# First block's attention: the second score product with 128 rows, the keys' low parts kept in both halves

## The chip, the core and the metric

The kernel runs on one core of a Trainium2 chip. Its engines run in parallel, each through its own instructions in order: TensorE (PE; the loading of its weights is shown as PEld), VectorE (DVE), ScalarE (ACT), GpSimd (POOL) and SyncE (SP, which issues the DMAs). They wait for each other by semaphores. The metric is device microseconds of one execution, the median of several runs. Lower is better.

## What is computed

256 latent tokens `x` and 256 context tokens `ctx`, of width 1024, go through a first block of two layers, then the latents alone through a second block (forgetting attention, an LRU, a mixture of 32 experts). Each layer of the first block has three branches, merged under gates:

```
s = einsum('btgrd,blgd->bgrtl', q, k) * 64 ** -0.5      # 2 key heads g, 4 query heads r for each
p = softmax(s, axis=-1)
y_attn = einsum('bgrtl,blgd->btgrd', p, v) * silu(a_g)
y_gla  = gla_finish(forward scan + backward scan) * silu(g_g)
mixed  = einsum('gts,bnsgc->bntgc', w_s, layer_norm(s_v)) + b_s
y_sgu  = s_u * mixed * silu(s_g)
m   = sigmoid(m_a) * (y_attn @ w_br_attn) + sigmoid(m_g) * (y_gla @ w_br_gla) + sigmoid(m_s) * (y_sgu @ w_br_sgu)
out = m @ w_out
```

Latents attend to the context and themselves (512 keys), context tokens to the context alone (256 keys). The second layer needs only the latents' output. All is fp32.

## The kernel before

Every fp32 operand of a large product is split into a high and a low part, and a product is made as high by high, high by low and low by high; lines 228, 229 and 230 are these three for one tile of a weight (`whi`, `wlo`) and of the transposed activations (`hTh`, `hTl`), with as many columns as there are tokens (512 in layer 0, 256 in layer 1). Lines 97 and 98 split the weights.

A layer runs its branches and then the merge, and a scheduler sets each engine's order: it takes an instruction when its inputs and its buffer are there by its own estimate. Buffers come from rings that are given out in the order of the program's text, a ring's next user waits for the one as many places before it as the ring has buffers. So work of a later function can stand between the steps of an earlier one wherever it has its inputs and buffers. The text's order in a layer ends with the GLA scan (`gops`, its finish with L846 on POOL and the transposes `tro`, L849), `attn_core`, `sgu_core`, and `merge`.

*Attention* (`attn_core`): for each tile of 128 queries (four in layer 0: two of latents, two of context; two in layer 1) four rounds `r` of two heads `g`. A round makes the scores `asc` in two PSUM banks, each by two products: the queries' high and low halves, stacked in `qs` over 128 rows, by the keys' high part `kh`, which is kept in both halves of the rows (L609); and the queries' high half by the keys' low part `kl`, over 64 rows (L611). Then come the maximum (L616, DVE), the exponential (L619, ACT), the division (L620, L621, DVE), four transposes (`trp`, L624, PE), their copy (`pt`, L626, ACT) and the weighting of the values (`aops`, L631, PE). After four rounds the tile is gated as `yt` (L635, DVE), and split into `yat`.

*SGU* (`sgu_core`): four products `mxps` for each tile of 128 tokens (L913), in a bank of the PSUM ring "gm", which has two; DVE takes them out into `mx` (L917, four instructions), POOL multiplies (L920), ACT and DVE split the result into `ysg` (L921, L922).

*Merge* (`merge`): twelve steps, each with gate products `mgps`, which need only the layer's input, and branch products `brps`. Their banks come from the same ring "gm" (in layer 1's attention steps the branch products take another).

In layer 1, POOL also prepares the residual with the layer norm's constants `post`, between the two heads of the last GLA pair (L1132, L1133), when they have been loaded.

Of the kernel before, what the change touches and what calls it, by code (L numbers as in the profile page):

```python
# [10 lines left out]
F32 = mybir.dt.float32  # L11
F32R = mybir.dt.float32r
# [3 lines left out]
OP = mybir.AluOpType  # L16
# [59 lines left out]
class Builder:  # L76
# [409 lines left out]
    def attn_tiles(self):  # L486
        L = self.L
        a1 = self.slot.tile([128, 2, 4, self.nx], F32, tag=self.half, bufs=self.nhalf, name="a1")
        L["a1"] = a1
        L["qT"], L["agT"] = a1[:, 0], a1[:, 1]  # L490

        L["kh"] = self.akv.tile([128, 2, 512], F32R, tag="kh", name="kh")
        L["kl"] = self.akv.tile([128, 512], F32R, tag="kl", name="kl")
        L["v"] = self.akv.tile([128, 4, 128], F32, tag="v", name="v")

    def attn_kv(self, t0, t1):
        nc, a, L = self.nc, self.a, self.L
        kh, kl, v = L["kh"], L["kl"], L["v"]
        tts = range(t0 // 128, t1 // 128)
        g = self.gemm_tok(self.chunk(a["w_in"][self.li], C_AK), tts)  # L500
        for tt in tts:
            kt = self.att.tile([128, 512], F32, tag="att2k", name="ktok")[:, :128]
            nc.scalar.activation(v[:, tt], g[tt][:, 128:256], AF.Copy)
            self.norm_rope(g[tt][:, 0:128], 2, 1, tt, kt.rearrange("p (h e) -> p h e", e=64))
            ps = self.ptr.tile([128, 128], F32, tag="tr", name="trk")
            nc.tensor.transpose(ps, kt, self.ident)
            ts = slice(tt * 128, tt * 128 + 128)
            for h in range(2):
                pr, other = slice(64 * h, 64 * h + 64), slice(64 - 64 * h, 128 - 64 * h)
                nc.scalar.activation(kh[pr, h, ts], ps[pr], AF.Copy)  # L510
                nc.vector.tensor_tensor(kl[pr, ts], ps[pr], kh[pr, h, ts].bitcast(F32), op=OP.subtract)
                nc.gpsimd.tensor_copy(kh[other, h, ts], kh[pr, h, ts])

    def attn_q(self):
        nc, a, L = self.nc, self.a, self.L
        w = a["w_in"][self.li]
        nq = self.nx // 128
        a1, qT = L["a1"], L["qT"]
        qtok = {}
        for c in range(2):  # L520
            g = self.gemm_tok(self.chunk(w, C_AQ + 256 * c), range(nq))
            for tt in range(nq):
                if c == 0:
                    qtok[tt] = a1[:, 1].rearrange("p r t -> p (r t)")[:, 512 * tt:512 * tt + 512].rearrange(
                        "p (r g e) -> p r g e", r=4, g=2)
                self.norm_rope(g[tt], 4, 0, tt, qtok[tt][:, :, c])
        for tt in range(nq):
            ps = self.ptr.tile([128, 4, 128], F32, tag="tr", name="trq")
            for r in range(4):
                nc.tensor.transpose(ps[:, r], qtok[tt][:, r].rearrange("p g e -> p (g e)"), self.ident)  # L530
            nc.scalar.activation(qT[:, :, tt * 128:tt * 128 + 128], ps, AF.Copy)
# [57 lines left out]
    def attn_core(self):  # L589
        nc, L = self.nc, self.L  # L590
        nq = self.nx // 128
        qT, kh, kl, v = L["qT"], L["kh"], L["kl"], L["v"]
        halves = [slice(64 * g, 64 * g + 64) for g in range(2)]
        y = L["y_a"] = self.slot.tile([128, 2, 4, self.nx], F32R, tag="slot", name="yat")
        for tt in range(nq):
            keys = (0, 512) if tt < 2 else (256, 512)
            nk = keys[1] - keys[0]
            nkc = nk // 128
            ops = self.pou.tile([128, 4, 128], F32, tag="ou", name="aops")

            qs = self.att.tile([128, 4, 2, 128], F32R, tag="qs", name="qs")
            for g in range(2):
                src, hi = qT[halves[g], :, tt * 128:tt * 128 + 128], qs[halves[g], :, g]
                nc.scalar.activation(hi, src, AF.Copy)
                nc.vector.tensor_tensor(qs[halves[1 - g], :, g], src, hi.bitcast(F32), op=OP.subtract)
            for r in range(4):
                sc = [self.psc.tile([128, 512], F32, tag="sc", name="asc")[:, :nk] for g in range(2)]
                for g in range(2):
                    nc.tensor.matmul(sc[g], qs[:, r, g], kh[:, g, keys[0]:keys[1]], start=True, stop=False)  # L609
                for g in range(2):  # L610
                    nc.tensor.matmul(sc[g], qs[halves[g], r, g], kl[halves[g], keys[0]:keys[1]], start=False, stop=True)  # L611
                pts = []
                for g in range(2):
                    s = sc[g]
                    st = self.sm.tile([128, 4], F32, tag="ast", name="ast")
                    nc.vector.tensor_reduce(st[:, 0:1], s, axis=AX.X, op=OP.max)  # L616
                    nc.vector.tensor_scalar(st[:, 1:2], st[:, 0:1], -0.125, None, op0=OP.mult)
                    p = self.att.tile([128, 512], F32, tag="att2k", name="p")[:, :nk]
                    nc.scalar.activation(p, s, AF.Exp, scale=0.125, bias=st[:, 1:2], accum_out=st[:, 2:3])  # L619
                    nc.vector.reciprocal(st[:, 3:4], st[:, 2:3])  # L620
                    nc.vector.tensor_scalar(p, p, st[:, 3:4], None, op0=OP.mult)  # L621
                    tp = self.ptr.tile([128, 4, 128], F32, tag="tr", name="trp")
                    for k in range(nkc):
                        nc.tensor.transpose(tp[:, k], p[:, k * 128:k * 128 + 128], self.ident)  # L624
                    pt = self.att.tile([128, 4, 128], F32, tag="pt", bufs=2, name="pt")
                    nc.scalar.activation(pt[:, :nkc], tp[:, :nkc], AF.Copy)  # L626
                    pts.append(pt)

                for k in range(nkc):
                    for g in range(2):  # L630
                        nc.tensor.matmul(ops[halves[g], r], v[:, keys[0] // 128 + k, 64 * g:64 * g + 64], pts[g][:, k],  # L631
                                         start=(k == 0), stop=(k == nkc - 1), skip_group_check=True)
            t = self.tmp.tile([128, 4, 128], F32, tag="tmp", name="yt")
            tc = slice(tt * 128, tt * 128 + 128)
            nc.vector.scalar_tensor_tensor(t, ops, 0.5, L["agT"][:, :, tc], op0=OP.mult, op1=OP.mult)  # L635
            nc.scalar.activation(y[:, 0, :, tc], t, AF.Copy)
            nc.vector.tensor_tensor(y[:, 1, :, tc], t, y[:, 0, :, tc].bitcast(F32), op=OP.subtract)
# [269 lines left out]
    def sgu_core(self):  # L907
        nc, L = self.nc, self.L
        y = L["y_s"]
        for tt in range(self.nx // 128):  # L910
            ps = self.pgm.tile([128, 4, 128], F32, tag="gm", name="mxps")
            for g in range(4):
                nc.tensor.matmul(ps[:, g], L["vn"][:, tt, g * 128:g * 128 + 128], L["wsT"][:, g], start=True, stop=True,  # L913
                                 skip_group_check=True)
            t = self.att.tile([128, 4, 128], F32, tag="mx", bufs=1, name="mx")
            for g in range(4):
                nc.vector.scalar_tensor_tensor(t[:, g], ps[:, g], L["vT"][:, 28 + g:29 + g], L["sgr"][:, g],  # L917
                                               op0=OP.mult, op1=OP.add)
            tc = slice(tt * 128, tt * 128 + 128)
            nc.gpsimd.tensor_tensor(t, t, L["su"][:, :, tc], op=OP.mult)  # L920
            nc.scalar.activation(y[:, 0, :, tc], t, AF.Copy)  # L921
            nc.vector.tensor_tensor(y[:, 1, :, tc], t, y[:, 0, :, tc].bitcast(F32), op=OP.subtract)  # L922
# [1048 lines left out]
```

## Time and profile before

| | before |
|---|---|
| median of 3 runs | 1337.82 us (1337.48 to 1339.54) |
| the profiled execution | 1342.17 us, span 1339.8 us |
| granted TensorE clock, mean | 0.981 |
| busy in the span | PE 1262.4 us (94%), DVE 724.2 (54%), ACT 577.9 (43%), POOL 334.9 (25%) |

The span is from the first to the last instruction of the profiled execution; busy is the time in which an engine had an instruction in work. A matmul's shown duration is longer than the distance to the next one, since they are pipelined; the distance of the starts tells what one costs.

### The profile page before, as it was taken

Reading aid. Unit: us, or ns where it says so; the run is one execution under the profiler, and the core shown is the slowest. Engines: PE = TensorE matmul, PEld = TensorE weight load, DVE = VectorE, ACT = ScalarE, POOL = GpSimd, SP = SyncE. Lnnn points to the kernel's source line nnn. Section 1 sums busy time; section 2 is a strip of 40 time slices with the busy share of each in tenths; the row PEclk is TensorE's granted clock in tenths of the full one; section 3 lists DMA queues with packets and bytes.
Section 4 is the critical chain, followed back from the end, with each engine's and each line's share of the span. In section 5 each row is a group of like instructions: output and inputs, shape, how many; then the busy total and the mean of one; then the engine's idle time right before and its main releaser. Section 6 shows DMA issues by size and latency. Waiting matters only on the chain.

```text
span 1339.8 us, 22959 instructions
## 1 busy us (share of the span) xinstructions
PE 1262.4 (94%) x8819; PEld 977.2 (73%) x8819; DVE 724.2 (54%) x1428; ACT 577.9 (43%) x1115; POOL 334.9 (25%) x373
## 2 busy tenths in 40 slices
PE   6999999999999999999999999999899989999975
PEld 3789888777777766799989988799898675333311
DVE  2565585775443323378768877646878455111112
ACT  2463454455343222346776554545465333222201
POOL 2237645340001101242246545002124020000000
PEclk9999999999999999999999999999899799999998
DMA  9613222211124676545555546246498546999994
GB/s 320 188 53 110 74 58 79 65 48 48 48 75 132 188 252 221 173 149 167 152 149 157 138 116 186 67 126 193 123 327 252 187 174 257 409 408 409 408 409 185
DMA packets 182165, 243.89 MB, mean 182 GB/s; under 512 B 15284, under 2 KB 154780, under 8 KB 182048
## 3 DMA queue, kind: packets, MB, share of 16 engines
q1 hardware_dynamic: 182048, 242.35, 54.9%
q8 instruction: 71, 1.16, 0.4%
q14 instruction: 46, 0.38, 0.1%
HBM read 241.27 MB, written 1.05 MB: 181 GB/s over the span
## 4 chain that ended last, share of the span: by engine, by line
PE 65%; DMA 15%; DVE 8%; ACT 4%; issue 3%; POOL 2%; SPq 1%; ACTq 0%; DVEq 0%; POOLq 0%
DMA gu<-w_up 7%; PE mgps L228 5%; PE mgps L230 5%; PE mgps L229 5%; PE gmt L263 4%; PE gmt L264 4%; PE gmt L265 4%; PE gups L1737 3%; DVE wlo L98 2%; DMA dn<-w_down 2%; DMA raw<-w_in 2%; PE brps L228 2%; PE brps L229 2%; PE brps L230 2%; PE aops L631 2%
## 5 line engine op out<-in xcount | busy, mean ns | idle before, releaser
L98 DVE TENSOR_TENSOR wlo<-raw,whi 128x1024 fp32r<-128x1024 f32 (+1 forms) x202 | 253.5, 1261 | 156.7 <-ACT whi L97 153.8
L97 ACT ACTIVATE whi<-raw 128x1024 fp32r<-128x1024 f32 (+1 forms) x216 | 212.5, 993 | 199.3 <-PE mgps L229 41.8
L264 PE MATMUL gmt<-wlo,hTh 128*128 128x256 f32 x480 | 138.0, 288 | 2.5 <-DVE wlo L98 2.5
L263 PE MATMUL gmt<-whi,hTh 128*128 128x256 f32 x480 | 137.3, 287 | 2.1 <-DVE a L587 0.9
L265 PE MATMUL gmt<-whi,hTl 128*128 128x256 f32 x480 | 137.3, 286 | 0.0
L228 PE MATMUL mgps<-hTh,whi 128*128 128x512 f32 (+1 forms) x384 | 132.0, 345 | 0.0
L229 PE MATMUL mgps<-hTl,whi 128*128 128x512 f32 (+1 forms) x384 | 130.6, 340 | 0.0
L230 PE MATMUL mgps<-hTh,wlo 128*128 128x512 f32 (+1 forms) x384 | 130.4, 342 | 0.0
L957 POOL TENSOR_TENSOR msum<-msum,tanh 128x512 f32<-128x512 f32 (+1 forms) x32 | 36.8, 1154 | 329.7 <-DVE tanh L956 310.2
L1737 PE MATMUL gups<-gu,xw 128*64 128x512 f32 (+1 forms) x512 | 97.5, 603 | 8.4 <-DMA gu<-w_up 8.4
L264 PEld LDWEIGHTS gmt<-wlo,hTh 128*128 128x128 f32 x480 | 92.6, 193 | 5.9 <-DVE wlo L98 2.9
L263 PEld LDWEIGHTS gmt<-whi,hTh 128*128 128x128 f32 x480 | 92.5, 193 | 3.9 <-ACT g L669 1.1
L265 PEld LDWEIGHTS gmt<-whi,hTl 128*128 128x128 f32 x480 | 92.7, 193 | 2.3 <-issue 2.2
L228 PEld LDWEIGHTS mgps<-hTh,whi 128*128 128x128 f32 x384 | 72.6, 189 | 12.9 <-issue 5.0
L230 PEld LDWEIGHTS mgps<-hTh,wlo 128*128 128x128 f32 x384 | 72.5, 189 | 10.2 <-issue 2.5
L229 PEld LDWEIGHTS mgps<-hTl,whi 128*128 128x128 f32 x384 | 72.7, 189 | 9.0 <-issue 2.0
L1737 PEld LDWEIGHTS gups<-gu,xw 128*64 128x64 f32 (+1 forms) x512 | 25.3, 124 | 62.0 <-issue 60.0
L203 POOL TENSOR_TENSOR frs<-rsq,mhalf 128x1 f32<-128x1 f32 x2 | 1.1, 549 | 234.7 <-DVE frs L1911 234.7
L1769 DVE SCALAR_TENSOR_TENSOR eth<-eth,gups 128x256 f32<-128x256 f32 x12 | 5.1, 421 | 99.8 <-ACT eth L1768 99.8
L1792 PE MATMUL dnps<-dn,hm 128*64 128x512 f32 (+1 forms) x256 | 52.2, 599 | 6.2 <-DMA dn<-w_down 6.0
L264 PE MATMUL gmt<-wlo,mm 128*128 128x256 f32 x192 | 54.5, 285 | 0.6 <-DVE wlo L98 0.6
L263 PE MATMUL gmt<-whi,mm 128*128 128x256 f32 x192 | 54.1, 285 | 0.0
(559 smaller groups left out, 3109.2 us busy)
## 6 DMA issues: line engine op xcount, KB each, us to landing
raw<-w_in SPq DMA_DIRECT2D x132, 512.0 KB
gu<-w_gate SPq DMA_DIRECT2D x64, 512.0 KB
gu<-w_up SPq DMA_DIRECT2D x64, 512.0 KB
dn<-w_down SPq DMA_DIRECT2D x28, 1024.0 KB
adar<-w_ada SPq DMA_DIRECT2D x32, 512.0 KB
raw<-w_out SPq DMA_DIRECT2D x32, 512.0 KB
adaw<-w_ada SPq DMA_DIRECT2D x16, 512.0 KB
raw<-w_in SPq DMA_DIRECT2D x32, 256.0 KB
```

Of the source, the lines that this page charges most:

```text
L97: nc.scalar.activation(hi, x, AF.Copy)
L98: return (eng or nc.vector).tensor_tensor(lo, x, hi.bitcast(F32), op=OP.subtract).ins
L228: nc.tensor.matmul(ps, wh, xh, start=(u == 0 and k == 0), stop=False)
L229: nc.tensor.matmul(ps, wh, xl, start=False, stop=False)
L230: nc.tensor.matmul(ps, wl, xh, start=False, stop=(u == len(acts) - 1 and k == 3))
L263: nc.tensor.matmul(out[tt], xh, hi[:, j, :n], start=first, stop=False, skip_group_check=True)
L264: nc.tensor.matmul(out[tt], xh, lo[:, j, :n], start=False, stop=False, skip_group_check=True)
L265: nc.tensor.matmul(out[tt], xl, hi[:, j, :n], start=False, stop=last, skip_group_check=True)
L631: nc.tensor.matmul(ops[halves[g], r], v[:, keys[0] // 128 + k, 64 * g:64 * g + 64], pts[g][:, k], start=(k == 0), stop=(k == nkc - 1), ski ...
L957: nc.gpsimd.tensor_tensor(sums[c, j], sums[c, j], ts[j], op=OP.add)
L1737: mm = nc.tensor.matmul(u["ps"][pr], u["x"][:, k, pr], u["gu"][ei][k // 4][:, :, k % 4], start=(k == 0), stop=(k == 7), skip_group_check=T ...
L1792: mm = nc.tensor.matmul(ps[pr], hm[:, f, pr], dns[ei][:, f, 512 * hf:512 * hf + 512], start=(f == 0), stop=(f == 1), skip_group_check=True ...
```

## The change

The keys' low part `kl` gets the shape of `kh`: each head's part is written to its own half of the rows (L511) and copied by POOL to the other half. The second score product then takes all 128 rows of `qs` and of `kl`, so that the queries' low part times the keys' low part comes in as well, and it follows the first product of the same head, where before both heads' first products were written ahead of both second ones. The tile `mx` of the SGU moves from a buffer of its own in the pool "att" to the ring "tmp", which has three buffers and is also used by `yt` and by the GLA's `on`. Both score products now have line 611; lines 513 to 610 lie one further down.

```diff
--- before.py
+++ after.py
@@ -490,7 +490,7 @@
         L["qT"], L["agT"] = a1[:, 0], a1[:, 1]
 
         L["kh"] = self.akv.tile([128, 2, 512], F32R, tag="kh", name="kh")
-        L["kl"] = self.akv.tile([128, 512], F32R, tag="kl", name="kl")
+        L["kl"] = self.akv.tile([128, 2, 512], F32R, tag="kl", name="kl")
         L["v"] = self.akv.tile([128, 4, 128], F32, tag="v", name="v")
 
     def attn_kv(self, t0, t1):
@@ -508,8 +508,9 @@
             for h in range(2):
                 pr, other = slice(64 * h, 64 * h + 64), slice(64 - 64 * h, 128 - 64 * h)
                 nc.scalar.activation(kh[pr, h, ts], ps[pr], AF.Copy)
-                nc.vector.tensor_tensor(kl[pr, ts], ps[pr], kh[pr, h, ts].bitcast(F32), op=OP.subtract)
+                nc.vector.tensor_tensor(kl[pr, h, ts], ps[pr], kh[pr, h, ts].bitcast(F32), op=OP.subtract)
                 nc.gpsimd.tensor_copy(kh[other, h, ts], kh[pr, h, ts])
+                nc.gpsimd.tensor_copy(kl[other, h, ts], kl[pr, h, ts])
 
     def attn_q(self):
         nc, a, L = self.nc, self.a, self.L
@@ -606,9 +607,8 @@
             for r in range(4):
                 sc = [self.psc.tile([128, 512], F32, tag="sc", name="asc")[:, :nk] for g in range(2)]
                 for g in range(2):
-                    nc.tensor.matmul(sc[g], qs[:, r, g], kh[:, g, keys[0]:keys[1]], start=True, stop=False)
-                for g in range(2):
-                    nc.tensor.matmul(sc[g], qs[halves[g], r, g], kl[halves[g], keys[0]:keys[1]], start=False, stop=True)
+                    for kx in (kh, kl):
+                        nc.tensor.matmul(sc[g], qs[:, r, g], kx[:, g, keys[0]:keys[1]], start=(kx is kh), stop=(kx is kl))
                 pts = []
                 for g in range(2):
                     s = sc[g]
@@ -912,7 +912,7 @@
             for g in range(4):
                 nc.tensor.matmul(ps[:, g], L["vn"][:, tt, g * 128:g * 128 + 128], L["wsT"][:, g], start=True, stop=True,
                                  skip_group_check=True)
-            t = self.att.tile([128, 4, 128], F32, tag="mx", bufs=1, name="mx")
+            t = self.tmp.tile([128, 4, 128], F32, tag="tmp", name="mx")
             for g in range(4):
                 nc.vector.scalar_tensor_tensor(t[:, g], ps[:, g], L["vT"][:, 28 + g:29 + g], L["sgr"][:, g],
                                                op0=OP.mult, op1=OP.add)
```

The order of the instructions changes at other places than these lines. **Layer 0's attention, second query tile, on PE before** (L609 and L611 make scores, L624 transposes, L631 weights the values, L228 to L230 are a merge step's branch products; a number behind a name counts the tiles of a program):

```order
L631 MATMUL aops<-pt,v 64x128
L609 MATMUL asc<-kh,qs 128x512
L611 MATMUL asc<-kl,qs 128x512
L624 MATMUL trp<-ident,p 128x128 x4
L631 MATMUL aops<-pt,v 64x128 x7
L609 MATMUL asc<-kh,qs 128x512
L611 MATMUL asc<-kl,qs 128x512
L228 MATMUL brps<-ysg,whi 128x512
L229 MATMUL brps<-ysg,whi 128x512
L230 MATMUL brps<-ysg,wlo 128x512
```

and with the change, in the same query tile:

```order
L631 MATMUL aops<-pt,v 64x128
L611 MATMUL asc<-kh,qs 128x512
L611 MATMUL asc<-kl,qs 128x512
L624 MATMUL trp<-ident,p 128x128 x4
L631 MATMUL aops<-pt,v 64x128 x7
L611 MATMUL asc<-kh,qs 128x512
L611 MATMUL asc<-kl,qs 128x512
L631 MATMUL aops<-pt,v 64x128
L624 MATMUL trp<-ident,p 128x128 x4
```

No merge product stands between the attention's steps of layer 0 any more; they follow behind its last one.

**The end of layer 0's attention on DVE, with the change** (the last head's division, yt, the SGU's mx, memsets of the second block, yat, ysg):

```order
L620 RECIPROCAL ast<-ast 128x1
L621 TENSOR_SCALAR p<-p,ast 128x256
L635 SCALAR_TENSOR_TENSOR yt<-aops,a_531 128x512
L917 SCALAR_TENSOR_TENSOR mx<-mxps,vT,sgr 128x128 x8
L1270 MEMSET bd_w_a_6075 128x512
L1270 MEMSET bd_w_x_6079 128x512
L637 TENSOR_TENSOR yat<-yt,yat 128x4x128
L922 TENSOR_TENSOR ysg<-mx,ysg 128x4x128
L917 SCALAR_TENSOR_TENSOR mx<-mxps,vT,sgr 128x128 x4
L922 TENSOR_TENSOR ysg<-mx,ysg 128x4x128
```

Before, mx stood among the softmax's steps of the first query tile, on DVE:

```order
L616 TENSOR_REDUCE ast<-asc 128x1
L922 TENSOR_TENSOR ysg<-mx,ysg 128x4x128
L617 TENSOR_SCALAR ast<-ast 128x1
L917 SCALAR_TENSOR_TENSOR mx<-mxps,vT,sgr 128x128 x4
L620 RECIPROCAL ast<-ast 128x1
L616 TENSOR_REDUCE ast<-asc 128x1
L621 TENSOR_SCALAR p<-p,ast 128x512
```

All sixteen L917 of the layer went from among the attention's steps to behind its last yt.

**Layer 1, where the GLA ends and attention begins, on PE with the change**:

```order
L829 MATMUL gops<-S,qin 128x128 x4
L833 MATMUL gops<-g_6094,acc 128x128 x2
L611 MATMUL asc<-kh,qs 128x512
L611 MATMUL asc<-kl,qs 128x512
L611 MATMUL asc<-kh,qs 128x512
L611 MATMUL asc<-kl,qs 128x512
L849 MATMUL tro<-ident,on 128x128 x4
L624 MATMUL trp<-ident,p 128x128 x8
L631 MATMUL aops<-pt,v 64x128
```

and before, around the same tro, merge products for gates and for the GLA's branch:

```order
L229 MATMUL mgps<-hTl,whi 128x256
L230 MATMUL mgps<-hTh,wlo 128x256
L228 MATMUL brps<-ygl,whi 128x256
L849 MATMUL tro<-ident,on 128x128 x2
L624 MATMUL trp<-ident,p 128x128 x4
L229 MATMUL brps<-ygl,whi 128x256
L230 MATMUL brps<-ygl,wlo 128x256
```

The transposes tro of both heads now stand together behind the last gops and four score products, and ahead of every transpose of attention. What they wait for stands so **on POOL with the change** (on is the GLA's output by its gate, post the constants of the layer norm):

```order
L846 TENSOR_TENSOR on<-on,g_6094 128x256
L1132 TENSOR_TENSOR x_3747<-x_3747,post 128x1024 x2
L203 TENSOR_TENSOR ors<-rsq,mhalf 128x2
L1133 TENSOR_TENSOR x_3747<-x_3747,post 128x1024 x2
L846 TENSOR_TENSOR on<-on,g_6094 128x256
L1168 MEMSET r2T 128x4x3
L920 TENSOR_TENSOR mx<-mx,s_7281 128x512 x2
```

The first head's gate multiplication moved ahead of L1132; the second's still stands behind L1133.

## Rows read from the trace of the kernel before

**Rows 1.** The page, part 4: chain of waits, share of the span by engine.
```profile
PE 65%; DMA 15%; DVE 8%; ACT 4%; issue 3%; POOL 2%; SPq 1%; ACTq 0%; DVEq 0%; POOLq 0%
```

**Rows 2.** Windows: length, then busy us of PE, PEld, DVE, ACT, POOL; clock; DMA share.
```profile
280.50:396.20 115.70, 113.47 (x621) 82.03 (x619) 65.42 (x165) 52.79 (x120) 6.81 (x5) 1.00 0.19 54
778.00:805.50 27.50, 26.07 (x284) 23.14 (x284) 21.75 (x52) 14.80 (x32) 11.31 (x16) 0.94 0.34 97
805.50:881.30 75.80, 73.89 (x564) 61.66 (x562) 48.40 (x92) 37.26 (x72) 19.74 (x15) 1.00 0.42 125
```

**Rows 3.** The same windows, instructions of line 228 alone.
```profile
280.50:396.20 115.70, 35.05 (x88) 16.35 (x88) 1.00 0.19 54
778.00:805.50 27.50, 13.39 (x43) 8.72 (x43) 0.94 0.34 97
805.50:881.30 75.80, 32.23 (x112) 20.92 (x112) 1.00 0.42 125
```

**Rows 4.** Timeline of PE: start us, duration us; one score step in layer 0.
```profile
258.04 0.39 PE L230 MATMUL sgps<-hTh,wlo 128*128 128x512 f32 x1
258.27 0.40 PE L609 MATMUL asc<-kh,qs 128*128 128x512 f32 x1
258.59 0.49 PE L611 MATMUL asc<-kl,qs 64*128 64x512 f32 x1
259.02 0.50 PE L228 MATMUL sgps<-hTh,whi 128*128 128x512 f32 x1
259.35 0.40 PE L229 MATMUL sgps<-hTl,whi 128*128 128x512 f32 x1
```

**Rows 5.** Timeline of PE in layer 1, merge products.
```profile
809.50 0.28 PE L230 MATMUL mgps<-hTh,wlo 128*128 128x256 f32 x1
809.62 0.28 PE L228 MATMUL mgps<-hTh,whi 128*128 128x256 f32 x1
```

**Rows 6.** Copies of line 512: durations min/median/max, first and last start.
```profile
L512 POOL CAST kh<-kh x16: 285/290/1172, 108.5 to 705.5; 64x128 fp32r<-64x128 f32 x16
```

**Rows 7.** Timeline of PE in layer 0, one head's first products two rounds apart.
```profile
283.42 0.50 PE L609 MATMUL asc<-kh,qs 128*128 128x512 f32 x1
...
295.80 0.50 PE L609 MATMUL asc<-kh,qs 128*128 128x512 f32 x1 [0.37 <-ACT p L619]
```

**Rows 8.** Groups by line and shape on DVE, layer 0's attention; mean ns behind the busy time.
```profile
L616 DVE TENSOR_REDUCE ast<-asc 128x1 f32<-128x512 f32 x12 | 8.3, 692 | 10.2 <-PE asc L611 10.1
L621 DVE TENSOR_SCALAR p<-p,ast 128x512 f32<-128x512 f32 x14 | 7.6, 545 | 0.4
L616 DVE TENSOR_REDUCE ast<-asc 128x1 f32<-128x256 f32 x16 | 6.8, 425 | 20.6 <-PE asc L611 20.6
L621 DVE TENSOR_SCALAR p<-p,ast 128x256 f32<-128x256 f32 x16 | 5.5, 352 | 0.6
L620 DVE RECIPROCAL ast<-ast 128x1 f32<-128x1 f32 x30 | 4.7, 159 | 4.1 <-ACT p L619 3.8
L917 DVE SCALAR_TENSOR_TENSOR mx<-mxps,vT,sgr 128x128 f32<-128x128 f32 x16 | 4.5, 345 | 0.5 <-PE mxps L913 0.5
```

**Rows 9.** The same groups on ScalarE (ACT).
```profile
L619 ACT ACTIVATE p<-asc,ast 128x512 f32<-128x512 f32 x14 | 9.6, 686 | 3.2 <-DVE ast L617 3.2
...
L619 ACT ACTIVATE p<-asc,ast 128x256 f32<-128x256 f32 x16 | 7.6, 472 | 0.9 <-DVE ast L617 0.7
```

**Rows 10.** Timeline of POOL in layer 1 around the GLA's last gate.
```profile
811.74 4.77 POOL L1132 TENSOR_TENSOR x<-x,post 128x1024 f32<-128x1024 f32 x2 [3.63 <-DMA post<-post_ln_g]
816.47 1.71 POOL L846 TENSOR_TENSOR on<-on,g 128x256 f32<-128x256 f32 x1
...
824.49 1.72 POOL L846 TENSOR_TENSOR on<-on,g 128x256 f32<-128x256 f32 x1
```

**Rows 11.** Timeline of PE in layer 1, the last gops.
```profile
804.97 0.71 PE L833 MATMUL gops<-g,acc 128*128 128x128 f32 x4
```

**Rows 12.** Timeline of PE in layer 1, the second tro.
```profile
826.27 0.44 PE L849 MATMUL tro<-ident,on 128*128 128x128 f32 x2 [0.28 <-POOL on L846]
```

## The prediction

> **What bounds the kernel now.** I read the chain of waits first: TensorE is 65% of it, DMA 15%, VectorE (DVE) 8% [rows 1]. So time won or lost on TensorE (PE) in the first block's layers goes into the total, and since the DMA issues for the experts at the end follow the layers, whatever delays the layers delays them by as much.
>
> Then the windows by engine. The change touches three stretches: layer 0's attention (115.70 us), and layer 1's last gated-linear (GLA) steps (27.50 us) and attention (75.80 us). PE is busy in 113.47, 26.07 and 73.89 us of them [rows 2]. The reader is to see that PE is full, DVE is busy in little over half, and the granted clock is 1.00, 0.94 and 1.00 of the 2.4 GHz level. PE is full because the merge's products, which need nothing of attention, stand between attention's steps. The count of line 228 in the same stretches is 88, 43 and 112 [rows 3]; L229 and L230 run as often, so 264, 129 and 336 products. Their pitch is 0.23 us with 512 columns (258.04 to 258.27, [rows 4]) and 0.12 with 256 (809.50 to 809.62, [rows 5]). With 0.227 and 0.12 us these fillings take 59.9, 15.5 and 40.3 us. What is left is PE's own time for attention and the steps around it: 115.7 - 59.9 = 55.8, 27.5 - 15.5 = 12.0 and 75.8 - 40.3 = 35.5 us.
>
> **What the change removes.** The timeline of PE shows one 64-row product among 128-row ones [rows 4]. Starts follow each other at 0.23, 0.32, 0.43 and 0.33 us from 258.04 on, where a product among its like takes 0.227: about 0.10 before the 64-row product, 0.20 in it and behind it, and 0.10 one further on, 0.40 us in all. There are 48 such products (8 rounds of two heads with 512 keys, 8 with 256 keys in layer 0, 8 with 512 in layer 1). Some stand beside other changes of shape and keep part of it; about 43 would save 0.40: 17 us. That is a saving only as long as PE is what ends last.
>
> The Trainium skill, in "TensorEngine Tiling (Array Packing)", section "Key Properties", says that changing the tiling mode drains TensorE. The trace agrees, with those 0.40 us; by this rule alone the kernel gets faster, which is the rival of the other sign below.
>
> **What it adds.** 16 copies of 64x128 on GpSimd (POOL), like L512's 16 copies, whose median is 0.29 us [rows 6]: 4.6 us, done as the keys are made (from 108.5 us on), long before the first score at 258.27 [rows 4]. Nothing waits for them; without that cover they cost at most 0.29 us each. I take 0. The second product reads 128 rows of low parts, at the pitch of a 128-row product.
>
> **What it moves.** This decides. `mx`, the tile that takes the SGU's mixing out of PSUM, had a buffer of its own, and goes to the ring of three "tmp" buffers, which in program order it gets behind the attention's `yt` tiles. The order of DVE shows the outcome: every L917 now stands behind the last `yt`. Until then its inputs (mxps) hold both banks of the ring "gm". The merge's products take banks of this ring, so none of them can stand between attention's steps, and the order of PE has none there. They all follow the attention. The fillings cost what they cost, 59.9 and 40.3 us; what counts is how long attention takes unfilled, against the 55.8, 12.0 and 35.5 us above.
>
> *Layer 0.* The trace has one stretch without fillings: PE's first-product starts of the same head at 283.42 and, two rounds on, at 295.80 [rows 7], 6.2 us per round. In each round DVE also did four L917 of 0.345 and one pass for ysg, like the reduction over 512 columns of 0.69 [rows 8], 2.0 us that leave with the change. 6.2 - 2.0 = 4.2. Bounds: DVE alone needs for two heads 2 x (0.69 + 0.55) and four small steps of 0.16 [rows 8], 3.1 us, and the scores' banks cannot be given back faster, so 3.6; above, 6.2, if what sets the round is latency and not DVE. For 256 keys three passes per head shorten by 0.27, 0.19 and 0.21 [rows 8, 9], 0.67 per head, of which some 0.8 for a round, since two heads overlap in part: 3.4 (bounds 2.9 and 4.6).
> - First query tile: 4 x 4.2 = 16.8. In the second tile the order puts seven weighting products ahead of the next scores, which serializes; between 4.2 and 6.2 I take 5.0: 20. Third 4 x 3.4 = 13.6, fourth 12. Less 2 us that lie before 280.5: 60 us.
> - Tail before the first merge product can begin: yt, eight L917 (2.8), two memsets, yat and ysg, four more L917 (1.4); at about 0.69 a pass and 0.5 a memset: 7.5 us.
> - 67.5 against 55.8, less one that overlaps: **+11**.
>
> *Layer 1.* The GLA steps of the second pair, unfilled, wait for each other; I allow **+3** (from 0 to 6). Then the new order has on PE two heads' scores and `tro x4` behind the last gops, and nothing else. tro waits for POOL, which has in order: L846 for head 0, two L1132, a small step, two L1133, L846 for head 1. Before, L1132 began at 811.74, when its constants had landed, after 3.63 us of waiting, and the last L846 began at 824.49 and took 1.72 [rows 10]. The last gops stands at 804.97 (0.71 us), tro for head 1 at 826.27 [rows 11, 12]: 20.6 us, then covered by merge products, now bare. In the new order L846 for head 0 (1.71) stands ahead of L1132 in the time of the wait, and the pair of L1133 may run undisturbed: I take 17.5 (bounds 14.5, the POOL chain alone, and 20.6). Queued behind tro on PE are the first transposes, behind those all weighting; DVE and ScalarE stop at their steps on tro too. After that seven rounds at 4.2 and 2.6 for a first whose scores are done: 32; tail 2.3, tro 0.4. Sum 52.2 against 35.5: **+17**.
>
> **The sum.** 11 + 3 + 17 = +31, less about 1 for switches that stay saved beside the GLA products: +30. The profiled execution took 1342.2 us (span 1339.8), so 1372; it lies 4.4 above the median 1337.8, so **1368** on the median's footing.
>
> **The rivals.** (1) *PE remains the bound and the switches are saved*: 1338 - 17 = 1321. For it: rows 4, and the fullness of PE. Against it: the order; it would need merge products between attention's steps, and those need a bank of "gm". It decides as soon as the mixing's banks come free before the last yt. Chance 0.04. (2) *Nothing changes*, the saving and the loss of cover being equal: 1338, 0.03. (3) *Short chain*: 3.6 and 2.9 us per round, 14.5 for tro, no loss in the GLA steps. Layer 0 then loses 10 us less (4 x 0.6, 4 x 1.4, 4 x 0.5, 4 x 0.1), layer 1 also 10 less (7 x 0.6, 3 and 3): +30 - 20 = +10, 1348. For it: DVE's sum of 3.1; against it: that measured rounds were never near it. Chance 0.11. (4) *Long chain*: with every bound at its top (6.2 and 4.6 us per round, 20.6 for tro, 6 for the GLA steps) layer 0 loses 24 us more (4 x 2.0, 4 x 1.2, 4 x 1.2, 4 x 1.6) and layer 1 20 more (7 x 2.0, 3 and 3): 1412; half of that is 1390, and I put the case at 1395. For it: the 6.2 measured, and that PE, a third idle, may be granted a lower clock; the windows show 0.94 in the GLA stretch, 1.00 in the other two, with PE nearly full in all three [rows 2]. Chance 0.17. The likeliest case, 0.65, has its own range 1353 to 1386.
>
> The Trainium skill, in "TensorE: Matmul & The Clock Gate", section "HAM oscillation — how this bites in real kernels", says that idle gaps of TensorE let its clock fall back. It speaks against this change, since it empties PE; by it the time is that of the long chain, near 1400. No stretch of the trace before is empty enough to show it.
>
> **How the numbers follow.** What a measurement of this kernel can tell from no change is about 0.2%, 2.7 us. Faster: rival 1, 0.04. Same: 0.03. Slower: the rest, 0.93. The range reaches from the short chain to where most of the long chain lies: 1346 to 1397; left out are rivals 1 and 2 (0.07), half of 3 and a quarter of 4, together under 0.2.
>
> **What would show it.** Right: windows over layer 0's attention and layer 1's have no L228 to L230; PE is busy in them for some 60 to 75%; all L917 start after the last yt; PE waits at tro for some 15 us with POOL's L846 as the releaser; layer 0's attention stretch is 58 to 72 us. In the island, products of low parts follow at 0.23 us. Wrong if merge products do appear among the scores, if a round takes under 3.6 us, or if the granted clock falls to about 0.5 there.

## The result, and the profile after

| | before | changed |
|---|---|---|
| median | 1337.65 us (1335.20 to 1339.54, 4 runs) | 1355.31 us (1349.99 to 1360.69, 4 runs) |
| ratio | | 1.0134 (1.0095 to 1.0172) |
| span of the profiled execution | 1339.8 us | 1358.9 us |
| granted TensorE clock, mean | 0.981 | 0.966 |

The changed kernel is slower by 17.7 us. The forecast was 1368, +30, with a range from 1346 to 1397: the way and the range hold, the size was too large by 12 us.

Where the time went is read first from four starts on PE: the last `sgps` of a layer (the last product ahead of the SGU's mixing) and the last product of its merge, in the timeline of PE (start us, duration us). Before:

```profile
279.03 0.39 PE L230 MATMUL sgps<-hTh,wlo 128*128 128x512 f32 x1
...
569.00 0.39 PE L230 MATMUL brps<-yat,wlo 128*128 128x512 f32 x1
...
773.48 0.29 PE L230 MATMUL sgps<-hTh,wlo 128*128 128x256 f32 x1
...
931.41 0.28 PE L230 MATMUL brps<-yat,wlo 128*128 128x256 f32 x1
```

With the change:

```profile
273.30 0.39 PE L230 MATMUL sgps<-hTh,wlo 128*128 128x512 f32 x1
...
567.03 0.39 PE L230 MATMUL brps<-yat,wlo 128*128 128x512 f32 x1
...
771.60 0.28 PE L230 MATMUL sgps<-hTh,wlo 128*128 128x256 f32 x1
...
950.30 0.28 PE L230 MATMUL brps<-yat,wlo 128*128 128x256 f32 x1
```

Three differences stand in these eight rows. The first row is 5.7 us *earlier* with the change. From it to the merge's end layer 0 takes 293.7 us instead of 290.0, +3.7. Layer 1 takes 178.7 instead of 157.9, +20.8. With 0.1 between the layers, the changed kernel is 18.9 us later at the end of layer 1, and 19.1 at the end.

The windows over the changed attention answer to [rows 2] (after the length: busy us of PE, PEld, DVE, ACT, POOL; clock; DMA share; GB/s):

```profile
274.90:327.00 52.10, 47.24 (x348) 31.76 (x345) 41.13 (x129) 36.60 (x101) 1.27 (x1) 1.00 0.06 19
327.00:334.40 7.40, 2.84 (x22) 2.35 (x22) 6.53 (x18) 1.91 (x4) 2.50 (x2) 1.00 0.57 178
776.00:797.00 21.00, 13.74 (x161) 10.19 (x162) 15.25 (x45) 8.18 (x24) 8.61 (x16) 0.59 0.16 55
797.00:808.80 11.80, 0.71 (x4) 0.48 (x4) 1.03 (x4) 0.38 (x1) 10.59 (x6) 0.61 0.14 37
808.80:816.50 7.70, 7.62 (x35) 5.28 (x34) 2.38 (x7) 3.42 (x9) 0.00 (x0) 0.50 0.40 132
816.50:837.20 20.70, 20.03 (x157) 14.20 (x155) 16.11 (x46) 14.71 (x37) 0.00 (x0) 1.00 0.00 1
```

and of line 228 alone over the first of them, which answers to [rows 3]:

```profile
274.90:327.00 52.10, 0.00 (x0) 0.00 (x0) 1.00 0.06 19
```

Not one merge product is left between 274.9 and 327 us, where there were 88 of L228 in the corresponding stretch. The end of this attention on DVE shows what they waited for:

```profile
327.76 0.69 DVE L635 SCALAR_TENSOR_TENSOR yt<-aops,a 128x512 f32<-128x512 f32 x1 [1.72 <-PE aops L631]
328.37 2.15 DVE L917 SCALAR_TENSOR_TENSOR mx<-mxps,vT,sgr 128x128 f32<-128x128 f32 x8
```

The last yt begins at 327.76, the first L917 of the layer at 328.37, and the first merge product at 334.40, when a bank of "gm" is free again. PE waited 2.67 us for that, released by L917:

```profile
334.40 0.50 PE L228 MATMUL mgps<-hTh,whi 128*128 128x512 f32 x1 [2.67 <-DVE mx L917]
```

In layer 1 the chain at tro lies bare, as forecast. Waits of PE from 770 to 845 us (total, times, longest), and POOL in the same place, which answers to [rows 10]:

```profile
PE tro L849 <- POOL on L846: 12.1, 2, 11.1
```

```profile
796.08 0.72 POOL L846 TENSOR_TENSOR on<-on,g 128x256 f32<-128x256 f32 x1 [0.57 <-DVE ast L617]
797.73 4.64 POOL L1132 TENSOR_TENSOR x<-x,post 128x1024 f32<-128x1024 f32 x2 [0.94 <-DMA post<-post_ln_g]
...
803.00 4.64 POOL L1133 TENSOR_TENSOR x<-x,post 128x1024 f32<-128x1024 f32 x2
807.59 0.73 POOL L846 TENSOR_TENSOR on<-on,g 128x256 f32<-128x256 f32 x1
```

Head 1's gate, at 807.59, is behind L1132 and L1133; PE waits 12.1 us in all for the two gates, 11.1 of it for this one. PE's rows at the ends of these stretches (the first score product behind the last gops, the second tro, the first merge product):

```profile
793.73 0.77 PE L611 MATMUL asc<-kh,qs 128*128 128x512 f32 x1
...
808.37 0.69 PE L849 MATMUL tro<-ident,on 128*128 128x128 f32 x2 [11.09 <-POOL on L846]
...
843.83 0.54 PE L228 MATMUL mgps<-hTh,whi 128*128 128x256 f32 x1 [1.82 <-DVE mx L917]
```

The fifth window tells what came with it: behind the wait the granted clock is 0.50, its lower level of 1.2 GHz, until 816.5, and PE, busy 7.62 of 7.70 us, does at half speed what attention is waiting for. In the last of the six windows it is 1.00. It was low ahead of this wait as well: 0.50 from 780 to 796 us, behind a wait of 2.1 us in the GLA steps (up to 779.39), then 1.00 from 797 to 799, and 0.50 again from 800 on.

What the change was to remove did go. PE, with 128 rows, against [rows 4]:

```profile
253.78 0.39 PE L229 MATMUL sgps<-hTl,whi 128*128 128x512 f32 x1
254.01 0.40 PE L611 MATMUL asc<-kh,qs 128*128 128x512 f32 x1
254.25 0.39 PE L611 MATMUL asc<-kl,qs 128*128 128x512 f32 x1
254.48 0.40 PE L230 MATMUL sgps<-hTh,wlo 128*128 128x512 f32 x1
```

Starts follow each other at 0.23, 0.24 and 0.23 us, where 64 rows made 0.23, 0.32, 0.43 and 0.33.

### The profile page after: what moved, and what is told of

Same layout as the page of the kernel before. It is cut to its first block, busy times and chain, and to the rows that moved or that the text cites. A ratio compares the mean times of both kernels' runs of the same rounds, so it can differ in the third digit from the quotient of the medians.

```text
span 1358.9 us, 23023 instructions
## 1 busy us (share of the span) xinstructions
PE 1260.0 (93%) x8819; PEld 982.9 (72%) x8819; DVE 717.5 (53%) x1428; ACT 578.8 (43%) x1115; POOL 340.5 (25%) x389
## 4 chain that ended last, share of the span: by engine, by line
PE 66%; DMA 13%; DVE 8%; ACT 5%; issue 3%; POOL 3%; SPq 1%; ACTq 0%; DVEq 0%; POOLq 0%
DMA gu<-w_up 7%; PE mgps L228 5%; PE gmt L264 5%; PE gmt L263 5%; PE mgps L229 5%; PE gmt L265 5%; PE mgps L230 5%; PE gups L1737 3%; PE brps L228 2%; DMA dn<-w_down 2%; PE brps L229 2%; PE brps L230 2%; DVE wlo L98 2%; PE aops L631 2%; PE dnps L1792 2%
## 5 line engine op out<-in xcount | busy, mean ns | idle before, releaser
L98 DVE TENSOR_TENSOR wlo<-raw,whi 128x1024 fp32r<-128x1024 f32 (+1 forms) x202 | 243.5, 1210 | 200.2 <-ACT whi L97 199.2
L228 PE MATMUL mgps<-hTh,whi 128*128 128x512 f32 (+1 forms) x384 | 131.7, 344 | 4.5 <-DVE mx L917 4.5
L230 PE MATMUL mgps<-hTh,wlo 128*128 128x512 f32 (+1 forms) x384 | 129.9, 341 | 0.0
L228 PEld LDWEIGHTS mgps<-hTh,whi 128*128 128x128 f32 x384 | 74.0, 193 | 15.9 <-DVE mx L917 4.9
L230 PEld LDWEIGHTS mgps<-hTh,wlo 128*128 128x128 f32 x384 | 73.9, 193 | 8.8 <-issue 1.2
```

What stands on the lines that cost most here:

```text
L98: return (eng or nc.vector).tensor_tensor(lo, x, hi.bitcast(F32), op=OP.subtract).ins
L228: nc.tensor.matmul(ps, wh, xh, start=(u == 0 and k == 0), stop=False)
L230: nc.tensor.matmul(ps, wl, xh, start=False, stop=(u == len(acts) - 1 and k == 3))
```

## Experiments

Medians are of 5 to 12 runs; each ratio is to runs of the kernel before on the same chip, with its 95% interval. "mx over vn" stands for a place that costs nothing: the normalized values `vn` of a token tile are read for the last time by the four mxps products, and mx has the same size.

**1. The parts apart.** Three kernels: mx alone in the ring tmp; the kernel before with mx over vn; the changed kernel with mx over vn. The line taken out is that of the kernel before; the first one added is that of mx_only, the second that of mx_vn, and of kl_vn in the changed kernel:

```diff
-            t = self.att.tile([128, 4, 128], F32, tag="mx", bufs=1, name="mx")
+            t = self.tmp.tile([128, 4, 128], F32, tag="tmp", name="mx")
+            t = L["vn"][:, tt].rearrange("p (g d) -> p g d", d=128)
```

> The kernel before with mx alone moved to the ring tmp; the keys' low parts stay over 64 rows. Theory A (the place of mx takes the merge's products out of attention, and this is what costs): 1356 to 1364, since the changed kernel's loss of 18 us stays and the 64-row products lengthen the unfilled rounds a little. Theory B (the loss comes from the low parts over 128 rows, their copies on POOL or the new order of the score products): 1338, as before.

> The kernel before with mx written over the normalized values vn of the same token tile, which are read for the last time by the four mxps products; mx then waits for no buffer. Theory A: 1333 to 1339, merge products stay among attention's steps. Theory B: 1338. The run is the footing for the next one.

> The changed kernel with mx written over vn instead of the ring tmp: low parts over 128 rows, and merge products among attention's steps. Theory A with the switches priced at 0.40 us each: 17 us faster than before, 1321 (1318 to 1327). Theory B: 1350 to 1360, no gain against the changed kernel. If the switches were worth nothing on the path: 1338.

| | median us | ratio to before |
|---|---|---|
| mx_only | 1375.90 | 1.0281 (1.0244 to 1.0318) |
| mx_vn | 1333.12 | 0.9964 (0.9947 to 0.9982) |
| kl_vn | 1316.58 | 0.9845 (0.9821 to 0.9870) |

Theory A holds and B falls: the low parts over 128 rows, with their copies, make the kernel faster by 16 to 21 us in both places of mx, and the ring tmp makes it slower by about 39 with them (1355.31 against 1316.58) and by about 43 without (1375.90 against 1333.12). The four starts in kl_vn:

```profile
275.11 0.39 PE L230 MATMUL sgps<-hTh,wlo 128*128 128x512 f32 x1
...
551.52 0.39 PE L230 MATMUL brps<-yat,wlo 128*128 128x512 f32 x1
...
756.80 0.28 PE L230 MATMUL sgps<-hTh,wlo 128*128 128x256 f32 x1
...
907.07 0.28 PE L230 MATMUL brps<-yat,wlo 128*128 128x256 f32 x1
```

Against before, layer 0 takes 276.4 us (13.6 less) and layer 1 150.3 (7.6 less). Its windows over the attentions show PE full again, at full clock:

```profile
276.50:380.00 103.50, 103.16 (x621) 81.11 (x620) 66.60 (x163) 53.90 (x121) 6.99 (x5) 1.00 0.21 61
...
787.00:850.00 63.00, 60.91 (x496) 54.45 (x497) 46.95 (x90) 34.55 (x68) 18.83 (x13) 1.00 0.46 135
```

mx_only is 12 us above the top of what was expected. Its windows from 300 to 350 us show one reason:

```profile
300.00:327.00 27.00, 25.81 (x154) 15.99 (x153) 17.99 (x60) 15.61 (x43) 0.00 (x0) 0.89 0.00 1
327.00:350.00 23.00, 20.82 (x77) 12.72 (x77) 10.55 (x40) 8.62 (x28) 0.42 (x1) 0.50 0.05 13
```

The granted clock falls to 0.50 inside layer 0's attention, where the changed kernel has 1.00 up to 334.4 us.

**2. The shape alone.** kl_vn with 64 rows in the second product, all copies kept; the order of every engine's instructions is the same.

```diff
-                    for kx in (kh, kl):
-                        nc.tensor.matmul(sc[g], qs[:, r, g], kx[:, g, keys[0]:keys[1]], start=(kx is kh), stop=(kx is kl))
+                    nc.tensor.matmul(sc[g], qs[:, r, g], kh[:, g, keys[0]:keys[1]], start=True, stop=False)
+                    nc.tensor.matmul(sc[g], qs[halves[g], r, g], kl[halves[g], g, keys[0]:keys[1]], start=False, stop=True)
```

> The kernel kl_vn (1316.6) with the second score product over 64 rows again; the copies of the low parts and every engine's order stay as they are there, so only the shape differs. Theory A: the switches are worth about 16 us where PE is full, 1330 to 1334. Theory C: a part of the gain is the other order that the copies bring in layer 0's GLA (PE's wait for S of L766, 2.3 us, and the low clock behind it go), worth 5 us by the traces; the shape is worth the rest, 1325 to 1330. If the shape is worth nothing: 1317.

1331.54 us, ratio 0.9939 (0.9925 to 0.9954). With PE full the shape is worth 15.0 us by the medians, 12.6 by the ratios (0.9845 against 0.9939), and 11.4 by the spans (1326.5 against 1315.1): 0.24 to 0.31 us for each of the 48 products, not 0.40 for 43. In kl_vn the products with 256 columns start at 333.63, 333.75 and 333.87, at the pitch of the fillings.

The total doesn't tell theory A from theory C: 1331.5 lies in A's band, but the ratio 0.9939 on the 1337.3 us that kl_vn was held against gives 1329.1, in C's. The stretch that C speaks of does, and it is the 5.7 us of the first section. In layer 0's GLA, PE waited before for the state S (total, times, longest), and the clock fell behind the wait:

```profile
PE attps L807 <- DVE S L766: 2.3, 2, 1.5
```

```profile
163.00:170.00 7.00, 4.68 (x63) 3.90 (x61) 6.11 (x14) 3.72 (x11) 2.72 (x4) 0.66 0.27 77
170.00:178.00 8.00, 8.00 (x54) 6.32 (x56) 4.59 (x4) 2.97 (x5) 3.62 (x3) 0.87 0.25 66
```

In the changed kernel:

```profile
PE attps L807 <- DVE S L766: 0.2, 1, 0.2
```

```profile
163.00:170.00 7.00, 6.79 (x88) 5.43 (x87) 6.40 (x13) 5.42 (x14) 3.68 (x5) 1.00 0.28 78
```

and in kl64_vn, with 64 rows but with the copies:

```profile
163.00:170.00 7.00, 6.75 (x88) 5.38 (x87) 6.20 (x13) 5.95 (x15) 4.21 (x5) 1.00 0.30 78
```

So it is not the shape: with the copies the scheduler's order on DVE is another. The weight split L98 (two, 1.28 us) stood ahead of the update L766 that PE's attps wait for, and stands behind it now. Before, and in the changed kernel:

```profile
163.91 1.28 DVE L98 TENSOR_TENSOR wlo<-raw,whi 128x512 fp32r<-128x512 f32 x2
165.12 0.72 DVE L766 SCALAR_TENSOR_TENSOR S<-S,ebl,ups 128x128 f32<-128x128 f32 x2
```

```profile
163.80 0.73 DVE L766 SCALAR_TENSOR_TENSOR S<-S,ebl,ups 128x128 f32<-128x128 f32 x2
164.44 1.29 DVE L98 TENSOR_TENSOR wlo<-raw,whi 128x512 fp32r<-128x512 f32 x2
```

Layer 0's last sgps begins at 275.4 in kl64_vn, at 275.3 in kl_pair (experiment 7, 128 rows and the old pairing), and at 279.4 in mx_vn. What the first two share and the third lacks are the copies and the wider kl that they fill; no run has these alone.

**3. The layers apart.** The changed kernel with mx in the ring in one layer, over vn in the other (the edit of tmp_l0; tmp_l1 has 1 in place of 0).

```diff
-            t = self.tmp.tile([128, 4, 128], F32, tag="tmp", name="mx")
+            t = (self.tmp.tile([128, 4, 128], F32, tag="tmp", name="mx") if self.li == 0
+                 else L["vn"][:, tt].rearrange("p (g d) -> p g d", d=128))
```

> The changed kernel with mx in the ring tmp in layer 0 alone, over vn in layer 1. By the positions in the traces of the changed kernel and of kl_vn layer 0 lies 15.5 us apart at its end. Theory A: 1329 to 1333. If the loss were all in layer 1: 1317.

> The changed kernel with mx in the ring tmp in layer 1 alone, over vn in layer 0. By the same positions layer 1 is 27.7 us longer. Theory A: 1339 to 1344, so that this loss and that of layer 0's kernel add up to the 39 us between kl_vn and the changed kernel. If both layers cost alike: 1336.

tmp_l0 1331.11 us, 0.9931 (0.9909 to 0.9952); tmp_l1 1339.75 us, 1.0000 (0.9987 to 1.0013). Against kl_vn's medians the ring costs 14.5 us in layer 0 and 23.2 in layer 1, 37.7 together, of 38.7. By the ratios, each to the kernel before on its own chip, it is 11.5 and 20.7, 32.2 of 38.7; each ratio is known to about 3 us, so it isn't settled whether the two losses add up to the whole. Both layers lose, layer 1 more.

**4. The wait at tro.** First L1132 and L1133 of the changed kernel were only written behind the merge:

```diff
-                    for t in range(2):
-                        nc.gpsimd.tensor_tensor(x2[:, t], x2[:, t], pv[:, 0], op=OP.mult)
-                        nc.gpsimd.tensor_tensor(x2[:, t], x2[:, t], pv[:, 1], op=OP.add)
-                    pv = self.post_norm(1)
                     self.merge(iter(()))
+                    for t in range(2):
+                        nc.gpsimd.tensor_tensor(x2[:, t], x2[:, t], pv0[:, 0], op=OP.mult)
+                        nc.gpsimd.tensor_tensor(x2[:, t], x2[:, t], pv0[:, 1], op=OP.add)
+                    pv = self.post_norm(1)
```

> The changed kernel with layer 1's four POOL products by the layer norm's constants (L1132, L1133) written behind the merge, so that POOL gates the second GLA head at once. Theory A (PE's wait at tro, 12.1 us in the changed kernel's waits, is bare): 10 to 12 us faster than the changed kernel, 1343 to 1347. Rival: another wait takes its place, 1355.

1354.77 us, 1.0125 (1.0102 to 1.0149): no gain, but no test either. The scheduler put them between the two gates again, and the wait is the old one, 12.3 us, the longest 11.2.

Then they were held back until the last L846 is issued:

```diff
-            nc.gpsimd.tensor_tensor(on, on, L["gg"][:, :nch, hd * 128:hd * 128 + 128], op=OP.mult)
+            self.last_on = nc.gpsimd.tensor_tensor(on, on, L["gg"][:, :nch, hd * 128:hd * 128 + 128], op=OP.mult).ins
...
-                    for t in range(2):
+                    with tc.issue_after(self.last_on):
+                        for t in range(2):
```

> The changed kernel with layer 1's four POOL products by the layer norm's constants held back until POOL has gated the last GLA head; the kernel that only wrote them later left POOL's order as it was. Theory A (PE's wait at tro is bare): 10 to 12 us faster than the changed kernel, 1343 to 1347. Rival: the end of the DMA's or another wait takes its place, or the time is given back behind the merge, 1353 to 1356.

1348.23 us, 1.0068 (1.0044 to 1.0092), 7 to 9 us less than the changed kernel. The wait and POOL now:

```profile
PE tro L849 <- POOL on L846: 3.2, 2, 2.1
```

```profile
799.54 0.72 POOL L846 TENSOR_TENSOR on<-on,g 128x256 f32<-128x256 f32 x1 [0.93 <-DVE on L845]
800.22 4.67 POOL L1133 TENSOR_TENSOR x<-x,post 128x1024 f32<-128x1024 f32 x2
```

8.9 us of the wait are gone, and layer 1 takes 169.6 us (772.3 to 941.9) instead of 178.7. So the wait is bare, as theory A has it; a little under the expected 10 to 12 came, since 3.2 us of wait stay. (L1133 here is the line that was L1132.) The low clock did not go with the wait. Behind the second tro, now after 2.1 us instead of 11.1, it is 0.50 for as long as before:

```profile
800.40:808.00 7.60, 7.52 (x33) 5.39 (x34) 4.86 (x7) 2.97 (x8) 7.60 (x4) 0.50 0.00 0
```

**5. 64 rows in an unfilled attention.** The changed kernel with the edit of experiment 2.

> The changed kernel with the second score product over 64 rows again, the orders of all engines unchanged. Theory A as the prediction had it (an unfilled attention is set by the chain through DVE and ScalarE, where a switch costs at most 0.2 us in the chain of a head): at most 24 x 0.2 = 5 us more than the changed kernel, 1355 to 1361. Theory D (the drains leave TensorE with so little that its granted clock falls to 0.50, as in 327 to 350 us of the kernel with mx alone in the ring tmp): 1366 to 1376, with the clock at 0.50 in the later part of layer 0's attention.

1364.60 us (1354.60 to 1371.71), 1.0193 (1.0154 to 1.0232). By the ratios that is 8 us over the changed kernel, between the two theories; the intervals overlap. The traces show it in the rounds: one head's first products with 512 keys start at 278.10, 282.14 and 286.20, 4.05 us apart, where the changed kernel has 3.73 to 3.75. Its window from 300 us on shows no fall of the clock in layer 0:

```profile
300.00:327.00 27.00, 25.30 (x160) 15.82 (x159) 18.61 (x71) 17.40 (x54) 0.00 (x0) 1.00 0.00 1
```

So D fails for this kernel. By these values the shape costs less in the unfilled kernel (8 us) than where PE is full (11 to 15), but the intervals don't separate the two. Why mx_only's clock fell, with the same shapes and rounds of the same 4.05 us up to there, is open.

**6. The ring's order.** The changed kernel with the SGU ahead of attention:

```diff
-            self.attn_core()
             self.sgu_proj()
             self.sgu_core()
+            self.attn_core()
```

> The changed kernel with the SGU's projections and mixing written ahead of the attention in the program's text; mx stays in the ring tmp, and gets its buffers ahead of the yt tiles. Theory A (not the ring itself but its order does it): merge products among attention's steps in both layers, 1317 to 1328. If three shared buffers are too few however they are ordered: 1345 to 1355.

1333.88 us, 0.9965 (0.9945 to 0.9984): 21 us of the ring's 39 came back, less than expected. Layer 0 is filled again; its merge ends at 556.8, against 551.5 in kl_vn. Layer 1 is only in part: from the last sgps (761.5) to the merge's end (927.7) it takes 166.1 us, against kl_vn's 150.3 and the changed kernel's 178.7, and PE still waits for mx:

```profile
PE mgps L228 <- DVE mx L917: 7.2, 1, 7.2
```

There the tiles ahead of mx in the ring are the GLA's `on` instead of yt: L917 stands behind the last of them on DVE. So it is the order in the ring, not the number of its buffers alone, that layer 0's loss hangs on; in layer 1 this order puts mx behind other late tiles. The edit moves the SGU's projections in the text as well, and no run keeps the two apart.

**7. The pairing.** kl_vn with both heads' high products ahead of both low ones:

```diff
-                    for kx in (kh, kl):
-                        nc.tensor.matmul(sc[g], qs[:, r, g], kx[:, g, keys[0]:keys[1]], start=(kx is kh), stop=(kx is kl))
+                    nc.tensor.matmul(sc[g], qs[:, r, g], kh[:, g, keys[0]:keys[1]], start=True, stop=False)
+                for g in range(2):
+                    nc.tensor.matmul(sc[g], qs[:, r, g], kl[:, g, keys[0]:keys[1]], start=False, stop=True)
```

> The kernel kl_vn (1316.6) with both heads' high products ahead of both low ones, as in the kernel before. Theory A: 1314 to 1320, the pairing order does nothing by itself. If it were a part of the gain: 1322 or more.

1314.22 us, 0.9821 (0.9794 to 0.9848): the same as kl_vn within the intervals. kl_vn and this one are the fastest, by 21 and 24 us against before; mx_vn, kl64_vn, tmp_l0 and sgu_first come out ahead of the kernel before by 4 to 8 us.

## Why the prediction was right in kind and too large in size

- **What decides** (mx behind the last yt, the banks held, attention without fillings): right. The windows, the DVE rows and experiments 1 and 3 show it.
- **The rival on the other side**, 17 us saved with PE as the bound: its condition, merge products between attention's steps, is what kl_vn restores, and there the gain is 21 us, of which the shape is 11 to 15. The saving was real and the ring spent it.
- **The price of a switch**, 0.40 us each and 17 in all: 0.24 to 0.31, 11 to 15 in all.
- **Layer 0, +11**: measured +3.7. The term that was mis-sized is attention unfilled, 60 us in the forecast and 52.9 in the trace (274.9 to 327.76, the start of the last yt); the tail was 6.6 (327.76 to 334.40) instead of 7.5. PE's first products of one head in the changed kernel, at the ends of some rounds with 512 keys:

```profile
278.06 0.48 PE L611 MATMUL asc<-kh,qs 128*128 128x512 f32 x1
...
281.79 0.50 PE L611 MATMUL asc<-kh,qs 128*128 128x512 f32 x1
...
285.54 0.50 PE L611 MATMUL asc<-kh,qs 128*128 128x512 f32 x1
```

and with 256 keys, the first of the third and of the fourth query tile and the last of the fourth:

```profile
300.42 0.28 PE L611 MATMUL asc<-kh,qs 128*128 128x256 f32 x1
...
313.76 0.39 PE L611 MATMUL asc<-kh,qs 128*128 128x256 f32 x1
...
322.27 0.39 PE L611 MATMUL asc<-kh,qs 128*128 128x256 f32 x1
```

  A round with 512 keys took 3.73 us, next to the lower bound of 3.6, not 4.2. The second query tile took no more for each of its four (285.54 to 300.42, 14.9 us, where 20 was forecast): seven weighting products ahead of the scores cost nothing. The first took 10.6 us from 274.9 on, where 14.8 was forecast, since more than 2 us of it lay before. With 256 keys a round took 3.1 on average (300.42 to 322.27, seven rounds), between the bounds of 2.9 and 4.6: the third tile 13.3 us against 13.6, the fourth 14.0 up to the last yt against 12. The 4.2 was taken from a stretch with 64-row products, two in each round, and after64, which has them, makes 4.05; so 0.32 of the difference is their switches. The 5.0 of the second tile had no such row behind it. PE was busy in 47.24 of 52.10 us: unfilled attention runs close to PE's own work, and there was little to lose.
- **A term left out**: the 5.7 us that layer 0's GLA gains by another order on DVE. Nothing of the prediction spoke of that stretch; the other order was to be had beforehand, and so was the low clock in the trace before (0.66 and 0.87 from 163 to 178 us), but not that it would go.
- **Layer 1, +20**: measured +20.8. That the two are so close is luck, since the parts lie apart by more. The GLA steps took 17.6 us (776.15 to 793.73) where their own time before was 12.0, +5.6 instead of +3, with the clock at 0.59. From the last gops to the second tro it took 14.6 us (793.73 to 808.37), where 17.5 was forecast and 14.5 was the bound: POOL's L846 took 0.73 us instead of 1.72, and L1133 4.64 for two. Attention and tail then took 35.5 (808.37 to 843.83) against 34.7 forecast: rounds of 3.75 us there too, but with the first 7.7 us at half the clock.
- **The long chain** had the granted clock as a reason. The Trainium skill, in "TensorE: Matmul & The Clock Gate", section "HAM oscillation — how this bites in real kernels", says that idle gaps let the clock fall back. The trace agrees in layer 1 (0.59, 0.61 and 0.50 in three windows from 776 to 816.5). Layer 0's attention had hardly a gap (PE busy 47.24 of 52.10 us, the longest wait 0.7) and kept 1.00; behind the waits of 1.8 and 2.7 us at its end the clock was 0.51 from 335.4 to 338.8. The prediction said that no stretch of the trace before is empty enough to show a fall; the GLA stretch of experiment 2 is one, with 0.50 from 166 to 172 us behind waits of 0.8 and 1.5.
- **Signs named beforehand**: no merge product, all L917 behind the last yt, and 0.23 us from a low-part product to the next came true, and the stretch of 59.5 us up to the merge is in 58 to 72. PE's share in unfilled attention is 91% in layer 0, not 60 to 75%; shown durations overlap, so it says little. PE waits 12.1 us at tro, some 15 were named. One sign of being wrong, a clock of about 0.5, did come in layer 1's attention, for its first 7.7 us.

## What to carry to other kernels

Moving a tile to a shared ring to make room is no neutral edit: ask which tiles stand ahead of it in the ring, when the last of them is freed, and what else the waiting producer holds, here two PSUM banks without which the merge couldn't start. Read the new order of the engines first, then price what becomes bare; a chain that had cover is worth its own length, and its rounds are best measured where nothing else stands between them and no product has a shape that the change removes. For room, look for a tile whose last reader is the new one's producer: vn cost no byte, and turned 18 us of loss into 21 of gain.

## What was not expected of the hardware

Behind the second tro PE's granted clock was 0.50 for 7.7 us although PE was busy in 7.62 of them, and so it was in experiment 4 (7.52 of 7.60), where the wait was 2.1 us instead of 11.1. In layer 0's GLA before, two waits of 2.3 us in all went with 0.66 and 0.87 in the next 15 us: in that stretch a wait of 2.3 us stands beside 5.7 us of difference. L846 on POOL took 1.72 us before and 0.73 in the changed kernel, with the same operands. In the traces of seven kernels its multiplications over 256 columns took 1.59 to 1.72 us where a weight split L98 was already running on DVE as they began, as at 816.47 and 824.49 before, and 0.72 to 0.75 where none was; no run changes that alone.
